# The last head's steps of a two-layer hybrid backbone, placed ahead of the products that fill TensorE's time

## The chip, the cores and the metric

One Trainium2 chip, one core of it. The metric is the device time of one execution in microseconds (us), as the median of some runs. The profile is of one execution.

## What is computed

Two layers over 256 context tokens and 512 latent tokens of 1024 channels. Layer 0 is a gated linear recurrence with 16 heads in both directions (HGRN2), layer 1 a scanned recurrence with a short convolution (RG-LRU). Each layer normalises, applies a modulation, widens, mixes, gates with SiLU and adds a gated projection back to the stream. Cut to layer 0:

```
h  = rms(x, norm_g) * (1 + scale) + shift            # 768 x 1024, context and latent
q, v, zf, zb, g = split(h @ w_in, 5)                 # 16 heads of 128 each
f  = lb + (1 - lb) * sigmoid(z);  k = 1 - f          # per direction
S  = diag(prod f) S + (k * decay)^T v                # chunk by chunk, carried state
o  = scores(q, k, decay) v + (q * decay) S           # forward plus backward
r  = rms(o, norm_g_head) * silu(g)                   # per head
x  = x + gate * (concat_heads(r) @ w_out)            # context and latent
```

Layer 1 starts from the mean square of every channel of the new x, so all 16 heads' projections must be in x before it begins.

## The kernel before, in words

The stream x stays in SBUF as `x1`, channels on the partitions: 8 blocks of 128 channels by 768 tokens. Products that need full precision are done as three fp32r products, high by high, high by low and low by high; `mm3` (L307) issues them, and `Weights.split` (L118) makes the high part of each weight tile on ScalarE (L129) and the low part on VectorE (L130), from pools of three buffers each.

**One head of layer 0** is a generator, `hgrn(h, side)` (L429). `prep` (L418) has made `kd`, `QQ` and the first `kt` from the head's projections. Then come:

- `dg`, the diagonal products (L442), and seven levels. At each, VectorE multiplies `KK` in place by decay products (L502), forms the next decays `T` (L507) and multiplies `QQ` in place (L509); ScalarE gathers the next `kt` from `KK` and, at odd levels, `qt` from `QQ` (L416, L490, L491); TensorE makes the score products `lv` (L460) of 32 or 64 columns; VectorE puts the low levels' scores into `D` under a mask (L468).
- Transposes of `KK` (L519), state products `U` (L533), the state chain `S` on VectorE (L541), the outputs `o` (L565).
- The norm of the head and the gate. Heads 0 to 14 take the mean by a product with ones (L580) and a reciprocal on VectorE (L588 to L590). Head 15 goes through `rstd_of` (L255): `msv` (L262), `rv` (L265, L266), `rbv` (L272), with L593 and L595 on VectorE.
- The result, split into `rhi` and `rlo` (L598 to L604; named `r` for head 14, which uses another pool).

`rhi` and `rlo` stand in a pool with one buffer for each parity of the head: head 15's `rhi` takes the buffer of head 13's.

**The fill.** While one head's chain runs, TensorE is kept busy with other products: the projections of the next head (`in_item`, L358) and output products of earlier heads (`out_item`, L391). `interleave` (L156) takes one step of the chain, adds its weight, and emits fill until the fill's share of its total has caught up. For head 15 the fill is `in_item(15, 3)`, the gate projection of head 15 itself (two halves, evacuated by a sigmoid at L337 and a multiply at L341), and `out_item((12, 13, 14))`: 16 items, each of nine products of 384 columns in one PSUM bank: three for head 12, three for 13, three for 14. An add on VectorE (L405, `x <- o`) takes each into `x1` and frees the bank. All fill takes its PSUM from `dps`, four banks; the chain takes its from `aps`, four others. The output products of head 15 alone follow behind the loop (`out_item((15,))`, L730), then the norm of layer 1 (`msh`, L262) and its first projections (`rc`, `rl`).

**What sets the order.** Nobody writes the engines' queues by hand. Every instruction has a number, its place in program order, and the planner fills each engine's queue in the order of its own timing model: at each moment the engine gets, of the instructions that the model has ready, the one with the lowest number. Buffers of a pool are given out in the order in which the program asked for them. `tc.high_priority(n)` takes n from the numbers of what is emitted inside and puts the counter back on leaving. The kernel before uses it for the weight splits (100, L128) and, in layer 1, for some evacuations. On the chip each engine then runs its queue in order, with semaphores between engines.

Of the kernel before, what the change touches and what calls it, by code (L numbers as in the profile page):

```python
# [20 lines left out]
NH = 16  # L21
# [129 lines left out]
def run_all(gen):  # L151
    for _ in gen or ():
        pass


def interleave(main, weight, filler, total):  # L156

    done, n = 0.0, 0.0
    for w in main:
        n += w  # L160
        while filler is not None and done < total * min(1.0, n / weight):
            try:
                done += next(filler)
            except StopIteration:
                filler = None
    run_all(filler)


def build(tc, ins, out, plan):
# [188 lines left out]
    def in_item(h, ty):  # L358
        w = wget("in", h, ty)
        in_tiles(h, ty)  # L360
        for half, c in enumerate(halves):
            ps = dtile(f"in{h}_{ty}_{half}")[:, :HN]
            mm3(ps, hpairs(w, c, range(4)), last=False)
            yield 1960.0
            mm3(ps, hpairs(w, c, range(4, 8)), first=False)
            in_evac(h, ty, half, ps)
            yield 1960.0

    def v_item(g):
        for u in range(2):  # L370
            st[2 * g + u]["V"] = vp.tile([P, NC, P], F32, name=f"V{2 * g + u}", tag="V")
        pss = [dtile(f"v{g}_{b}") for b in range(3)]
        for part in range(2):
            whi, wlo = (w.rearrange("p (k e) -> p k e", k=4) for w in wget("v", g, part))
            for c in range(NC):
                t = slice(P * c, P * c + P)
                ps = pss[c // 2][:, 256 * (c % 2):256 * (c % 2) + 256]
                for k in range(4):
                    kk = 4 * part + k
                    for i, (xh, w) in enumerate(((h_hi, whi), (h_hi, wlo), (h_lo, whi))):  # L380
                        PE.matmul(ps, lhsT=xh[:, kk, t], rhs=w[:, k],  # L381
                                  start=part == 0 and k == 0 and i == 0 and c % 2 == 0,
                                  stop=part == 1 and k == 3 and i == 2 and c % 2 == 1, skip_group_check=True)
                if part == 1 and c % 2 == 1:
                    b = c // 2
                    src = pss[b].rearrange("p (c e) -> p c e", c=2)
                    for u in range(2):
                        A.activation(st[2 * g + u]["V"][:, 2 * b:2 * b + 2], src[:, :, P * u:P * u + P], AF.Copy)
                yield 1300.0

    def out_item(heads, accs=None, done=None):  # L391
        ws = [wget("out", h) for h in heads]
        gate = ada[0][:, 2]
        parts = segs if accs else halves
        order = [(d, i) for d in range(DK) for i in range(2)]
        for d, i in sorted(order, key=lambda x: x[1]) if accs else order:
            e = slice(P * d, P * d + P)
            c = parts[i]
            ps = dtile(f"o{heads[0]}_{d}_{i}")[:, :c.stop - c.start]
            mm3(ps, [(w[0][:, e], w[1][:, e], st[h]["r"][0][:, c], st[h]["r"][1][:, c]) for h, w in zip(heads, ws)])  # L400
            for j, g in enumerate(segs):
                a, b = max(c.start, g.start), min(c.stop, g.stop)
                if a < b:
                    xs = x1[:, d, a:b]
                    V.scalar_tensor_tensor(xs, ps[:, a - c.start:b - c.start], gate[:, d, 1 - j:2 - j], xs,  # L405
                                           ALU.mult, ALU.add)
            if accs:
                sumsq(accs, THREE, lambda n: ktp.tile([P, NT], F32, name=n, tag="kt"), d, c)
                if d == DK - 1:
                    done(i)  # L410
            yield 490.0 * len(heads)
# [6 lines left out]
    def prep(h):  # L418

        s = st[h]  # L420
        QQ = s["QQ"] = qqp.tile([P, 2, NT], F32, name=f"QQ{h}", tag="QQ")
        kd = s["kd"] = kdp.tile([P, NT], F32, name=f"kd{h}", tag="kd")
        kt = s["kt"] = ktp.tile([P, NT], F32, name=f"kt{h}_0", tag="kt")
        V.tensor_tensor(kd, s["KK"][:, 0], s["KK"][:, 1], ALU.add)
        gather(s["KK"], kt, 1)
        V.tensor_tensor(QQ[:, 0], s["q"], s["T0"][:, 1], ALU.mult)
        V.tensor_tensor(QQ[:, 1], s["q"], s["T0"][:, 0], ALU.mult)
# [179 lines left out]
    HW = 1.5 + 28.0 - 6.3 + 1.5 + 3.0 + 3.6 + 0.5 + 7.0  # L607
# [83 lines left out]
    def chain_(gens):  # L691
        for g in gens:
            yield from g

    def head_in(h):
        outs = out_item((h - 3, h - 2)) if h % 2 and h >= 3 else None
        yield from in_item(h, 0)
        yield from in_item(h, 1)
        yield from in_item(h, 2)
        prep(h)  # L700
        if h % 2 == 0:
            yield from v_item(h // 2)
        if h < NH - 1:
            yield from outs or ()
            yield from in_item(h, 3)

    def extra(h):
        if h in (1, 2):
            return [ada_block(0, 3 + h)]
        return [ada_block(1, h - 10)] if h >= 10 else []  # L710

    for h in range(NH):
        if h == 0:
            fill, total = [v_item(0), in_item(0, 3), head_in(1)], 54700.0
        elif h < NH - 1:
            fill, total = [head_in(h + 1)], 45300.0 if h < NH - 2 else 23500.0
        else:
            fill, total = [in_item(h, 3), out_item((h - 3, h - 2, h - 1))], 31400.0
        side = chain_(extra(h + 1) if h < NH - 1 else [])
        interleave(hgrn(h, side), HW, chain_(fill), total)  # L720
        run_all(side)
    accs1 = [pl.tile([P, n], F32, name=f"acc1_{i}", tag=t)[:, :NT]
             for i, (pl, t, n) in enumerate(((kdp, "kd", NT), (qp, "q", NT), (sp, "S", 2 * (NC - 1) * P)))]
# [306 lines left out]
```

## Time and profile before

| what | value |
|---|---|
| median of 3 runs | 1586.57 us (1585.46 to 1586.60) |
| the profiled execution, own time | 1585.53 us |
| its span in the profile | 1583.7 us |
| TensorE busy | 1530.8 us, 97% |
| VectorE busy | 1208.6 us, 76% |
| ScalarE busy | 903.9 us, 57% |
| granted TensorE clock, mean | 0.986 |
| share of TensorE in the chain that ended last | 87% |

The profile times start at the first instruction. A line of the timeline gives the start, the duration, the engine, the line of the kernel, the output and inputs by tile name, the number of merged instructions and, in brackets, the idle time of the engine just before and what ended it. On TensorE each 384-column product is shown with its full length of 0.34 us, but such products start some 0.17 us apart. Four-byte products of the chain are shown as two instructions each. The granted clock (PEclk) is 1.00 at 2.4 GHz and 0.50 at 1.2 GHz.

### The profile page before, as it was taken

To read this page: it belongs to the slowest core of one execution; us is meant where nothing else is said; L and a number is where in the kernel's file an instruction comes from. 1 tells how busy PE (TensorE), PEld (TensorE's weight loads), DVE (VectorE), ACT (ScalarE), POOL (GpSimd) and SP (SyncE) were. 2 spreads that over 40 slices of the span, in tenths; PEclk is the share of its full clock that TensorE was granted. 3 is DMA by queue.
4 is the path that set the end of the run, shared out by engine and by line. 5 is a ranking of instruction groups with operands and counts; after the bars stand their busy time and mean duration, and the time that the engine had idled before them with its cause. 6 is when DMAs were issued, how large, how long until landed. Compare 5 with 4: busy or idle time off the path is not lost.

```text
span 1583.7 us, 34061 instructions
## 1 busy us (share of the span) xinstructions
PE 1530.8 (97%) x14740; PEld 1429.7 (90%) x14740; DVE 1208.6 (76%) x1867; ACT 903.9 (57%) x1423; POOL 11.8 (1%) x16
## 2 busy tenths in 40 slices
PE   5999999999999999999999999998999999999995
PEld 3899999999999999999999999987888888888884
DVE  4767678768867878767866876787668797797898
ACT  4554554555544554554445555654578577667874
POOL 0000000000000000000000000001000000000001
PEclk9999999999999999999999999998999999999997
DMA  8231211111211211223222131201222212221211
GB/s 317 91 121 54 95 55 41 55 54 30 80 41 42 68 45 51 81 69 103 70 92 73 54 120 56 94 15 54 66 68 67 89 59 67 94 78 59 76 54 53
DMA packets 33861, 116.80 MB, mean 74 GB/s; under 512 B 3632, under 2 KB 6064, under 8 KB 33712
## 3 DMA queue, kind: packets, MB, share of 16 engines
q1 hardware_dynamic: 32192, 113.26, 22.5%
q8 instruction: 116, 1.90, 0.5%
q10 hardware_dynamic: 1520, 1.37, 0.3%
q14 instruction: 33, 0.27, 0.1%
HBM read 112.52 MB, written 2.10 MB: 72 GB/s over the span
## 4 chain that ended last, share of the span: by engine, by line
PE 87%; DVE 8%; ACT 2%; issue 1%; POOL 0%; DMA 0%; POOLq 0%; DVEq 0%; ACTq 0%
PE in L311 12%; PE in L312 11%; PE in L313 11%; PE v L381 9%; PE lv L460 4%; PE o L565 4%; PE r L313 3%; PE r L311 3%; PE r L312 3%; PE o L311 3%; PE o L312 3%; PE o L313 3%; PE U L533 2%; PE gt L311 2%; PE gt L312 2%; PE gt L313 2%
## 5 line engine op out<-in xcount | busy, mean ns | idle before, releaser
L311 PE MATMUL in<-h_hi,hi 128*128 128x384 f32 x1024 | 350.4, 343 | 3.4 <-ACT h_hi L304 2.8
L312 PE MATMUL in<-h_lo,hi 128*128 128x384 f32 x1024 | 345.8, 338 | 0.3 <-DVE h_lo L305 0.3
L313 PE MATMUL in<-h_hi,lo 128*128 128x384 f32 x1024 | 344.6, 337 | 0.0
L130 DVE TENSOR_TENSOR lo<-raw,hi 128x1024 fp32r<-128x1024 f32 x160 | 195.8, 1225 | 85.9 <-ACT hi L129 85.6
L129 ACT ACTIVATE hi<-raw 128x1024 fp32r<-128x1024 f32 x160 | 168.1, 1057 | 110.5 <-PE in L312 49.3
L311 PEld LDWEIGHTS in<-h_hi,hi 128*128 128x128 f32 x1024 | 192.9, 189 | 16.8 <-issue 9.9
L312 PEld LDWEIGHTS in<-h_lo,hi 128*128 128x128 f32 x1024 | 193.1, 189 | 2.8 <-issue 1.6
L313 PEld LDWEIGHTS in<-h_hi,lo 128*128 128x128 f32 x1024 | 192.6, 188 | 0.8 <-issue 0.4
L509 DVE TENSOR_TENSOR QQ<-QQ,T 128x768 f32<-128x768 f32 x112 | 117.7, 1051 | 20.7 <-ACT qt L491 20.5
L313 PE MATMUL r<-h_hi,lo 128*128 128x512 f32 (+1 forms) x344 | 123.8, 360 | 3.8 <-DVE lo L130 3.8
L416 ACT ACTIVATE kt<-KK 128x768 f32<-128x768 f32 x112 | 102.5, 915 | 40.8 <-DVE KK L502 33.1
L502 DVE TENSOR_TENSOR KK<-KK,T 128x768 f32<-128x768 f32 x112 | 117.3, 1047 | 9.7 <-ACT kt L416 8.2
L312 PE MATMUL r<-h_lo,hi 128*128 128x512 f32 (+1 forms) x344 | 123.1, 358 | 0.0
L311 PE MATMUL r<-h_hi,hi 128*128 128x512 f32 (+1 forms) x344 | 123.0, 358 | 0.0
L337 ACT ACTIVATE sg<-in 128x384 f32<-128x384 f32 x128 | 61.5, 482 | 100.7 <-PE in L313 100.5
L381 PE MATMUL v<-hi,h_hi 128*128 128x256 f32 x384 | 111.3, 290 | 0.0
L381 PE MATMUL v<-hi,h_lo 128*128 128x256 f32 x384 | 107.4, 280 | 0.0
L381 PE MATMUL v<-lo,h_hi 128*128 128x256 f32 x384 | 107.3, 279 | 0.0
L588 DVE RECIPROCAL sq<-sq 128x384 f32<-128x384 f32 x30 | 76.3, 2546 | 21.1 <-ACT sq L582 20.9
L405 DVE SCALAR_TENSOR_TENSOR x<-o,ada,x 128x256 f32<-128x256 f32 (+1 forms) x184 | 82.1, 486 | 11.3 <-PE o L313 10.8
L311 PE MATMUL o<-rhi,hi 128*128 128x384 f32 (+2 forms) x240 | 85.3, 357 | 1.8 <-DVE lo L130 1.2
L311 PE MATMUL gt<-xh,hi 128*128 128x384 f32 x256 | 85.6, 337 | 0.8 <-ACT xh L790 0.4
(207 smaller groups left out, 3280.1 us busy)
## 6 DMA issues: line engine op xcount, KB each, us to landing
raw<-in_hgw_dram SPq DMA_DIRECT2D x64, 512.0 KB, 3.6
raw<-in_ada_dram SPq DMA_DIRECT2D x48, 512.0 KB, 3.8
raw<-in_rgi_dram SPq DMA_DIRECT2D x32, 512.0 KB, 3.9
raw<-in_hgv_dram SPq DMA_DIRECT2D x16, 512.0 KB, 3.5
raw<-in_hgo_dram SPq DMA_DIRECT2D x16, 512.0 KB, 3.6
raw<-in_rgg_dram SPq DMA_DIRECT2D x16, 512.0 KB, 3.6
raw<-in_rgo_dram SPq DMA_DIRECT2D x16, 512.0 KB, 3.9
x<-in_x_dram SPq DMA_DIRECT2D x8, 384.0 KB, 5.9
```

Source lines behind the costliest of these rows:

```text
L129: self.nc.scalar.activation(hi, r, AF.Copy)
L130: self.nc.vector.tensor_tensor(lo, r, hi.bitcast(F32), ALU.subtract)
L311: PE.matmul(ps, lhsT=wh, rhs=xh, start=first and i == 0, stop=False, skip_group_check=skip)
L312: PE.matmul(ps, lhsT=wh, rhs=xl, start=False, stop=False, skip_group_check=skip)
L313: PE.matmul(ps, lhsT=wl, rhs=xh, start=False, stop=last and i == n - 1, skip_group_check=skip)
L381: PE.matmul(ps, lhsT=xh[:, kk, t], rhs=w[:, k], start=part == 0 and k == 0 and i == 0 and c % 2 == 0, stop=part == 1 and k == 3 and i == 2 ...
L405: V.scalar_tensor_tensor(xs, ps[:, a - c.start:b - c.start], gate[:, d, 1 - j:2 - j], xs, ALU.mult, ALU.add)
L416: A.activation(view(kt, 0, [[2 * B, n], [B, 2], [1, B]]), view(KK, 0, [[2 * B, n], [NT + B, 2], [1, B]]), AF.Copy)
L460: PE.matmul(ps[w * g:w * g + w, w * c:w * c + w], lhsT=kt[:, o:o + w], rhs=rhs, start=c == 0, stop=c == NC - 1, skip_group_check=True, til ...
L502: V.tensor_tensor(kv, kv, view(T, 1, [[2, n], [m - 1, 2], [0, B]]), ALU.mult)
L509: V.tensor_tensor(qv, qv, view(T, m + 1, [[2, n], [-m - 1, 2], [0, B]]), ALU.mult)
L588: V.reciprocal(rs, rs)
```

## The change

A new generator wraps the head's generator and takes each of its steps inside `tc.high_priority(2000)`. It is used for head 15 alone. The fill of head 15, everything of head 14, the projections and `prep` of head 15 and the weight splits keep their numbers. No instruction is added, removed or resized.

```diff
+    def ahead_of_fill(gen):
+
+        while True:
+            with tc.high_priority(2000):
+                w = next(gen, None)
+            if w is None:
+                return
+            yield w
+
@@
         side = chain_(extra(h + 1) if h < NH - 1 else [])
-        interleave(hgrn(h, side), HW, chain_(fill), total)
+        interleave(hgrn(h, side) if h < NH - 1 else ahead_of_fill(hgrn(h, side)), HW, chain_(fill), total)
         run_all(side)
```

## Rows read from the trace of the kernel before

**Rows 1.** The page: TensorE and VectorE; busy us, share, instructions.
```profile
PE 1530.8 (97%) x14740; PEld 1429.7 (90%) x14740; DVE 1208.6 (76%) x1867; ACT 903.9 (57%) x1423; POOL 11.8 (1%) x16
```

**Rows 2.** Stretches: length; PE, PEld, DVE, ACT, POOL busy (instructions); PEclk; DMA share, GB/s.
```profile
1030.30:1035.00 4.70, 4.47 (x114) 3.76 (x113) 4.66 (x6) 4.47 (x6) 0.00 (x0) 1.00 0.01 3
1035.00:1040.00 5.00, 3.06 (x69) 2.49 (x71) 5.00 (x8) 2.43 (x4) 0.00 (x0) 1.00 0.34 97
1040.00:1045.00 5.00, 4.08 (x112) 3.68 (x113) 5.00 (x12) 1.73 (x3) 0.00 (x0) 1.00 0.03 11
1045.00:1056.00 11.00, 11.00 (x170) 9.77 (x169) 10.89 (x24) 7.15 (x15) 0.00 (x0) 1.00 0.01 1
1060.00:1075.57 15.57, 15.57 (x109) 15.15 (x107) 6.88 (x19) 3.98 (x7) 0.00 (x0) 1.00 0.01 2
1075.57:1080.00 4.43, 1.73 (x10) 1.32 (x10) 4.43 (x6) 3.06 (x4) 0.00 (x0) 0.99 0.53 143
1080.00:1084.00 4.00, 3.98 (x17) 3.47 (x17) 4.00 (x9) 2.62 (x7) 2.67 (x3) 0.59 0.47 156
1091.00:1104.00 13.00, 10.29 (x49) 9.76 (x48) 9.88 (x18) 5.90 (x11) 2.28 (x2) 0.61 0.11 40
```

**Rows 3.** VectorE by line, 1029.4 to 1056 us; busy us, mean ns, idle.
```profile
L509 DVE TENSOR_TENSOR QQ<-QQ,T 128x768 f32<-128x768 f32 x7 | 7.3, 1049 | 0.1
L502 DVE TENSOR_TENSOR KK<-KK,T 128x768 f32<-128x768 f32 x7 | 7.3, 1045 | 0.0
L405 DVE SCALAR_TENSOR_TENSOR x<-o,ada,x 128x256 f32<-128x256 f32 (+2 forms) x14 | 6.0, 470 | 0.0
L507 DVE TENSOR_TENSOR T<-T 128x768 f32<-128x768 f32 (+6 forms) x7 | 2.6, 379 | 0.0
L468 DVE COPY_PREDICATED D<-masks,lv 128x192 f32<-128x192 uint8 x5 | 1.8, 365 | 0.0
L341 DVE SCALAR_TENSOR_TENSOR gs<-in,prm,sg 128x384 f32<-128x384 f32 x2 | 1.2, 603 | 0.0
L130 DVE TENSOR_TENSOR lo<-raw,hi 128x1024 fp32r<-128x1024 f32 x1 | 1.2, 1202 | 0.0
L604 DVE TENSOR_TENSOR r<-sq,r 128x384 fp32r<-128x384 f32 x1 | 0.9, 909 | 0.0
```

**Rows 4.** VectorE's timeline: start us, us, line, op, out<-in.
```profile
1029.44 0.94 DVE L424 TENSOR_TENSOR kd<-KK 128x768 f32<-128x768 f32 x1
1030.77 1.63 DVE L502 TENSOR_TENSOR KK<-KK,T 128x768 f32<-128x768 f32 x1
...
1035.87 1.20 DVE L130 TENSOR_TENSOR lo<-raw,hi 128x1024 fp32r<-128x1024 f32 x1
...
1055.06 1.26 DVE L405 SCALAR_TENSOR_TENSOR x<-o,ada,x 128x384 f32<-128x384 f32 x3
...
1073.34 0.69 DVE L595 TENSOR_TENSOR gs<-gs,rbv 128x512 f32<-128x512 f32 x1 [1.41 <-PE rbv L272]
```

**Rows 5.** TensorE's timeline, 1036 to 1079 us.
```profile
1036.84 0.63 PE L460 MATMUL lv<-qt,kt 128*32 128x32 f32 x48 [1.59 <-ACT qt L416]
1037.39 0.61 PE L313 MATMUL o<-r,lo 128*128 128x384 f32 x2
...
1075.06 0.34 PE L312 MATMUL o<-r,hi 128*128 128x384 f32 x1
1075.23 0.34 PE L313 MATMUL o<-r,lo 128*128 128x384 f32 x1
...
1078.23 0.38 PE L312 MATMUL o<-rlo,hi 128*128 128x256 f32 x1 [0.86 <-DVE rlo L599]
```

**Rows 6.** ScalarE's timeline.
```profile
1041.26 0.85 ACT L416 ACTIVATE kt<-KK 128x768 f32<-128x768 f32 x1 [1.92 <-DVE KK L502]
...
1074.39 2.00 ACT L129 ACTIVATE hi<-raw 128x1024 fp32r<-128x1024 f32 x2 [2.67 <-PE o L312]
1076.30 0.40 ACT L598 ACTIVATE rhi<-gs 128x256 fp32r<-128x256 f32 x1
```

## The prediction, made before the change was run

> **What bounds the kernel now.** I read the engines' shares first: TensorE is busy 97% of the span, VectorE 76% [rows 1]. So an edit pays only where TensorE stands idle, and the place to look is the stretch of head 15. The view of busy time by stretch [rows 2] shows three parts. From 1030.3 to 1045 TensorE is idle 0.23 + 1.94 + 0.92 = 3.1 us, while VectorE is full. From 1045 to 1056 and from 1060 to 1075.57 TensorE is full. From 1075.57 to 1080 it works 1.73 of 4.43 us.
>
> Next, what ends the first part. VectorE by line [rows 3] has two kinds of work in it. The chain of head 15: 7.3 + 7.3 + 2.6 + 1.8 = 19.0 us. The rest are things that the fill needs: the last steps of head 14's result (L590, L604), the low part of head 14's output weights (L130), the gate multiply that empties the two banks of head 15's gate projection (L341), and the adds that empty the output banks (L405). All eleven lines of that view (L424, L589 and L590, 1.9 us together, are not shown) make 30.2 us in 26.6 us of time, because neighbours overlap; so a listed microsecond costs 0.88.
>
> Last, what ends the stretch. The last fill product starts at 1075.23 and ends at 1075.57 [rows 5], and head 15's last multiply is over at 1073.34 + 0.69 = 1074.03 [rows 4], before it. Two things of the tail wait for the fill, not for the chain. Head 15's `rhi` takes head 13's buffer, which the fill reads to its last item, and it runs at 1076.30 [rows 6]. And the split of head 15's output weights takes head 12's buffer; it starts at 1074.39 after a wait for an output product [rows 6]. **So a chain that is done earlier lets nothing start earlier.** The stretch ends when TensorE has done its fill, and its end moves by what TensorE's idle time before that does.
>
> **What the change moves.** No work is added. The four windows from 1030.3 to 1056 and the one from 1060 hold 574 TensorE and 69 VectorE instructions [rows 2]; 2000 is more than twice that, so head 15's steps go ahead not of the fill alone but of everything that is left of head 14 and of the weight splits, on TensorE, VectorE and ScalarE alike, wherever they are ready. On POOL and in the DMA queue the chain has nothing; no weight load moves by itself, but each one waits for the split that frees its buffer, and those go back with the rest.
>
> *VectorE.* The chain's first multiply needs `kd` (L424), which is not raised: it ends about 1030.3 [rows 4]. From there the chain's 19.0 us take 19.0 x 0.88 = 16.7 us if nothing comes between: the levels end near 1047.0, against the 1055.06 at which the adds behind the last level start now [rows 4]. Does anything come between? A gather is 0.85 us [rows 6] and stands between two multiplies of `KK`, which with the 0.95 of the multiply and some 0.1 us for each hand-over makes 2.0 us a level; VectorE's own work is 16.7 / 7 = 2.4 us a level on average, somewhat less at the last levels, where `T` is small. So VectorE has hardly a gap before the last levels, and L590, L604, L130 and most of L341 wait till then. This is the step on which the forecast rests.
>
> *TensorE.* Of an output item the first six products need heads 12 and 13 only; the third three need head 14's result, and its low product also the weights' low part: today two such products stand behind L130 until 1037.39 [rows 4, 5]. Of the four banks two are held by the gate projection until L341 has run for each half. So with VectorE withheld, the fill has 2 banks x 6 products, 0.17 us apart [rows 5], that is 2.1 us. The chain's own products are eight bundles, 0.63 us each [rows 5], 5.0 us in all. From 1031.3 to 1047 that is 7.1 us of work in 15.7 us: idle 8.6. Bounds: the 3.1 us of today if VectorE finds room for the fill's helpers after all (0 more; less than that is rival A), and 8.6 us (5.5 more). I take 8.0, since some helpers slip in at the last levels: 8.0 - 3.1 = **+4.9 us**. Behind the levels the transposes, states and outputs of head 15 cover the (0.9 + 1.2 + 1.2) x 0.88 = 2.9 us that VectorE then needs for L604, L130 and L341 [rows 3]; if that cover fails, it is up to 2.9 us more.
>
> *The waits that go.* The 1.59 us in front of the score product [rows 5] is a wait for the chain; it is inside the 3.1 us subtracted above.
>
> *The clock.* Behind the stretch with 1.73 us of work in 4.43, the granted clock is 0.59 over 4 us [rows 2], that is 0.41 / 0.5 x 4 = 3.3 us at the lower of the two levels, 1.2 GHz. From 1091 it is 0.61 over 13 us, 10.1 us at the lower level [rows 2]. From 1035 to 1040, with 3.06 of 5 us busy, it stayed at 2.4 GHz. While TensorE starves, the lower level costs little; behind that, where its queue is full again, it costs half of the time that it lasts: bounds 0 and 10.1 / 2 = 5 us. The row of 1080 is the nearest, as it too follows a few microseconds of broken work, and I take half of its 3.3 us: **+1.7 us**. The Trainium skill ("TensorE: Matmul & The Clock Gate", Part 1, What's actually happening) says that the throttled state is the default and that activity releases it; by that the loss is certain and the time 1592.7, by the row of 1035 there is none and the time 1591.0. The rows of 1080 and 1091 are with the page.
>
> *The tail.* ScalarE runs two splits (2.00 us) and then `rhi` [rows 6]; with the change `rhi` passes the second, 1.0 us sooner behind the end of the fill, and the 0.86 us wait for `rlo` [rows 5] shrinks. But the second split's VectorE half then stands in front of the adds that empty the banks. Bounds -1.0 and 0; I take **-0.5 us**.
>
> Sum: 4.9 + 1.7 - 0.5 = +6.1 us on the profiled execution's 1585.53 us: 1591.6. The median of the runs shown is 1.04 us above that execution; against it the forecast is **1592.7 us**, 0.4% slower. The times below are against the median too.
>
> **The rivals.** A: *the chain's lead counts*, faster. If head 14's result, the low part of its weights and the emptied gate banks stand in VectorE's queue before head 15's first multiply, the fill is fed throughout; the 3.1 us of idle time, which end mostly with chain steps, go, and the tail gives 1.0: -4.1, 1582.5 us. The point that decides is whether L604 and L130 come before L502's first. For it: the largest of today's gaps, 1.59 us, ends with a gather of the chain [rows 5], which then comes sooner. Against it: L130 is at 1035.87 now, behind that multiply at 1030.77 [rows 4], and the change only pushes it back. The Trainium skill ("Perfetto Trace Analysis", Optimization Strategy) says to find the gaps on the engine one optimizes for and to make what ends them start sooner or finish faster; this rival is that rule at work, and it leaves out what the raised steps push back. Chance 0.10.
>
> B: *nothing that can be measured*, because VectorE has gaps enough (the gather paces the levels, 2.0 us against 2.4 is not far), or because the order is fixed by readiness and 2000 changes little: idle 3.1 us as now, tail -0.5 to 0: 1586.1 to 1586.6 us. Chance 0.16.
>
> C: *the clock stays low* through the transposes, states, outputs and much of the fill: with twice the 10.1 us of 1091 to 1104 at the lower level it costs +10.1 instead of +1.7, 1601.1 us. The row of 1091 is for it, the 3.3 us at 1080 against it [rows 2]. Chance 0.08.
>
> **How the numbers follow.** The forecast has 0.66, and reaches from the least that counts as slower to 5.5 + 5 + 0 us, 1597.1. A measurement of this kernel can tell about 0.2%, 3.2 us, from no change. Slower than that: the forecast and C, 0.74. Within: B, 0.16. Faster: A, 0.10. The range reaches from 1586.0, B's time, to 1600.0, just short of C.
>
> **What would show it.** In the changed kernel's trace: L502 seven times by about 1047 with hardly an L405 between; L604 of `r` and L130 of head 14's weights behind 1040; TensorE some 40 to 60% busy between 1032 and 1046 with score products alone; a granted clock below 1 somewhere from 1035 to 1060; the last fill product near 1081; head 15's last multiply near 1060, 20 us before `rhi`. It is wrong if L604 stays near 1032, or if TensorE is as full as now in 1030 to 1045.

## The result, and the profile after

| | before | after |
|---|---|---|
| median of 6 runs each | 1585.51 us (1583.69 to 1586.60) | 1597.06 us (1595.32 to 1598.21) |
| ratio, 95% interval | | 1.007 [1.006, 1.008] |
| the profiled execution, own time | 1585.53 us | 1598.0 us |
| its span | 1583.7 us | 1596.2 us |
| TensorE busy | 1530.8 us | 1537.6 us |
| granted clock, mean | 0.986 | 0.981 |
| last fill product starts | 1075.23 | 1086.34 |
| first `rc` product of layer 1 starts | 1096.04 | 1108.96 |

The change made the kernel 11.5 us slower; 6.1 had been forecast. Of the 12.9 us by which the profiled execution is late at layer 1, 11.1 are there when the fill ends.

The page's first part of the changed kernel, where [rows 1] has 1530.8 and 1208.6: TensorE is busy 6.8 us longer with as many instructions, so not all of the loss is idle time.

```profile
PE 1537.6 (96%) x14740; PEld 1434.6 (90%) x14740; DVE 1210.0 (76%) x1867; ACT 903.4 (57%) x1423; POOL 11.8 (1%) x16
```

Stretches of the changed kernel, the columns as in [rows 2]: length, then TensorE, its weight loads, VectorE, ScalarE and POOL busy, granted clock, DMA share, GB/s.

```profile
1030.30:1035.00 4.70, 2.65 (x59) 2.04 (x58) 4.63 (x7) 3.44 (x5) 0.00 (x0) 0.96 0.28 94
1035.00:1040.00 5.00, 4.73 (x105) 4.19 (x105) 5.00 (x8) 4.07 (x6) 0.00 (x0) 0.50 0.06 20
1040.00:1045.00 5.00, 2.19 (x160) 1.87 (x148) 4.79 (x9) 2.51 (x4) 0.00 (x0) 0.84 0.01 3
1045.00:1050.00 5.00, 2.87 (x67) 2.18 (x58) 4.65 (x7) 4.35 (x11) 0.00 (x0) 0.50 0.02 3
1050.00:1055.00 5.00, 5.00 (x24) 3.96 (x23) 0.69 (x2) 1.93 (x6) 0.00 (x0) 0.50 0.00 0
```

Three things are to be seen. TensorE is idle 2.05 + 0.27 + 2.81 + 2.13 = 7.3 us from 1030.3 to 1050, where it was 3.1 [rows 2]. The clock is at its lower level, 1.2 GHz, in most of 1035 to 1055, where it was at 2.4 GHz throughout. And from 1050 to 1055 TensorE is full with 24 instructions, while VectorE does 0.69 us of work: something else than VectorE makes it slow there.

VectorE's timeline of the changed kernel (start, duration, engine, line, operation, out<-in, count, idle time before), where [rows 4] has the first `L502` at 1030.77:

```profile
1031.06 1.23 DVE L130 TENSOR_TENSOR lo<-raw,hi 128x1024 fp32r<-128x1024 f32 x1
1032.21 1.59 DVE L502 TENSOR_TENSOR KK<-KK,T 128x768 f32<-128x768 f32 x1
1033.65 0.53 DVE L590 TENSOR_TENSOR sq<-sq,gs 128x384 f32<-128x384 f32 x1
1034.11 0.93 DVE L426 TENSOR_TENSOR QQ<-q,T 128x768 f32<-128x768 f32 x1
...
1046.53 0.95 DVE L502 TENSOR_TENSOR KK<-KK,T 128x768 f32<-128x768 f32 x1
1047.40 0.95 DVE L509 TENSOR_TENSOR QQ<-QQ,T 128x768 f32<-128x768 f32 x1
1048.27 0.86 DVE L604 TENSOR_TENSOR r<-sq,r 128x384 fp32r<-128x384 f32 x1
1049.03 0.62 DVE L341 SCALAR_TENSOR_TENSOR gs<-in,prm,sg 128x384 f32<-128x384 f32 x1
...
1060.21 1.26 DVE L405 SCALAR_TENSOR_TENSOR x<-o,ada,x 128x256 f32<-128x256 f32 x3
```

The seven `L502` stand between 1032.21 and 1046.53 with no add (`L405`) between them. Head 14's last `L604` goes from 1032.44 to 1048.27, the first add from 1042.48 to 1060.21.

TensorE's timeline of the changed kernel. The first two lines are waits for the chain; the next four are score products of the last level and state products, taking turns; the last two are the end of the fill and head 15's first product with `rlo`, which [rows 5] has at 1075.23 and 1078.23:

```profile
1043.27 0.63 PE L460 MATMUL lv<-qt,kt 128*32 128x32 f32 x48 [2.21 <-ACT qt L416]
...
1046.95 1.28 PE L460 MATMUL lv<-qt,kt 128*32 128x32 f32 x48 [1.77 <-ACT qt L490]
...
1055.21 0.33 PE L460 MATMUL lv<-QQ,kt 128*64 128x64 f32 x2
1055.47 0.49 PE L533 MATMUL U<-V,KK 128*128 128x128 f32 x2
1055.89 0.33 PE L460 MATMUL lv<-QQ,kt 128*64 128x64 f32 x2
1056.15 0.49 PE L533 MATMUL U<-V,KK 128*128 128x128 f32 x2
...
1086.34 0.34 PE L313 MATMUL o<-r,lo 128*128 128x384 f32 x1
...
1088.20 0.38 PE L312 MATMUL o<-rlo,hi 128*128 128x256 f32 x1 [0.67 <-DVE rlo L599]
```

And ScalarE's at the end of the fill: the split of head 15's weights has waited 17.32 us for the fill's products, and `rhi` runs behind it, 16 us after the chain's last multiply (1070.39).

```profile
1085.49 1.06 ACT L129 ACTIVATE hi<-raw 128x1024 fp32r<-128x1024 f32 x1 [17.32 <-PE o L312]
1086.46 0.40 ACT L598 ACTIVATE rhi<-gs 128x256 fp32r<-128x256 f32 x1
```

### The profile page after: what moved, and what is told of

The parts are those of the page before. It is cut to its first block, busy times and chain, and to the rows that moved or that the text cites. A ratio compares the mean times of both kernels' runs of the same rounds, so it can differ in the third digit from the quotient of the medians.

```text
span 1596.2 us, 34068 instructions
## 1 busy us (share of the span) xinstructions
PE 1537.6 (96%) x14740; PEld 1434.6 (90%) x14740; DVE 1210.0 (76%) x1867; ACT 903.4 (57%) x1423; POOL 11.8 (1%) x16
## 4 chain that ended last, share of the span: by engine, by line
PE 87%; DVE 8%; ACT 3%; issue 1%; DMA 1%; POOL 0%; POOLq 0%; DVEq 0%; ACTq 0%
PE in L311 12%; PE in L312 11%; PE in L313 11%; PE v L381 9%; PE lv L460 4%; PE o L565 4%; PE r L313 3%; PE r L311 3%; PE r L312 3%; PE o L311 3%; PE o L312 3%; PE o L313 3%; PE U L533 2%; PE gt L311 2%; PE gt L312 2%; PE gt L313 2%
## 5 line engine op out<-in xcount | busy, mean ns | idle before, releaser
L130 DVE TENSOR_TENSOR lo<-raw,hi 128x1024 fp32r<-128x1024 f32 x160 | 196.0, 1226 | 85.8 <-ACT hi L129 85.5
L509 DVE TENSOR_TENSOR QQ<-QQ,T 128x768 f32<-128x768 f32 x112 | 117.9, 1053 | 20.7 <-ACT qt L491 20.5
L502 DVE TENSOR_TENSOR KK<-KK,T 128x768 f32<-128x768 f32 x112 | 117.8, 1051 | 9.7 <-ACT kt L416 8.2
L405 DVE SCALAR_TENSOR_TENSOR x<-o,ada,x 128x256 f32<-128x256 f32 (+1 forms) x184 | 82.4, 488 | 19.0 <-PE o L313 18.6
```

What stands on the lines that cost most here:

```text
L130: self.nc.vector.tensor_tensor(lo, r, hi.bitcast(F32), ALU.subtract)
L502: V.tensor_tensor(kv, kv, view(T, 1, [[2, n], [m - 1, 2], [0, B]]), ALU.mult)
L509: V.tensor_tensor(qv, qv, view(T, m + 1, [[2, n], [-m - 1, 2], [0, B]]), ALU.mult)
```

## The experiments

The theory behind the prediction: the raised levels take VectorE from what the fill needs, TensorE starves, and the lower clock adds to it. The rivals: the loss comes from the raised steps behind the levels; it comes from one overtaken piece only; or the clock costs nothing. All runs stand in one table. The comparisons ran on different chips, so "above before" and the ratio are each against the kernel before in the same comparison, and runs of different comparisons are compared by these. The fill's end is the start of its last product in the profiled execution, the idle time is the sum of the windows from 1030.3 to 1050.

| run | us | above before | ratio, 95% interval | fill's end | TensorE idle |
|---|---|---|---|---|---|
| before | 1585.5 | | | 1075.23 | 3.1 |
| the change | 1597.06 | 11.6 | 1.007 [1.006, 1.008] | 1086.34 | 7.3 |
| e1, levels | 1593.72 | 8.9 | 1.0051 [1.0037, 1.0065] | 1081.39 | 8.6 |
| e2, behind the levels | 1598.12 | 13.3 | 1.0077 [1.0063, 1.0091] | 1087.71 | 1.5 |
| e4, levels written first | 1592.07 | 7.2 | 1.0039 [1.0025, 1.0053] | 1080.76 | 7.9 |
| e3, ten products more | 1598.12 | 13.3 | 1.0076 [1.0062, 1.0091] | 1086.07 | 2.2 |
| e7, numbers in a row | 1595.03 | 10.2 | 1.0065 [1.0053, 1.0078] | 1084.37 | 9.5 |
| e10, e7 and four products | 1594.74 | 9.9 | 1.0064 [1.0051, 1.0076] | 1083.12 | 5.9 |
| e8, behind the levels, in a row | 1586.59 | 1.8 | 1.0005 [0.9996, 1.0014] | 1075.07 | 3.1 |
| e11, e7 and helpers raised | 1591.45 | 6.6 | 1.0047 [1.0035, 1.0060] | 1081.50 | 5.9 |
| e14, e11 and adds raised | 1586.81 | 1.5 | 1.0011 [1.0002, 1.0020] | 1074.40 | 1.2 |
| e5, before, free buffers | 1587.27 | 2.0 | 1.0011 [1.0002, 1.0020] | 1075.39 | 3.1 |
| e16, e8, free buffers | 1585.11 | -0.2 | 1.0000 [0.9991, 1.0009] | 1075.98 | 3.1 |
| e15, e14, free buffers | 1586.85 | 1.5 | 1.0009 [1.0000, 1.0017] | 1074.61 | 1.2 |

### Two halves, and a price that nobody had looked for

e1 raises the first seven steps, e2 those behind them; e2's line has `7 <= i < 99`.

```diff
-        while True:
-            with tc.high_priority(2000):
+        for i in range(99):
+            with tc.high_priority(2000 if 0 <= i < 7 else 0):
                 w = next(gen, None)
```

> Only the seven levels of head 15 are raised by 2000; its transposes, states, outputs and result keep their own priority. Theory 1 (the levels starve the fill, and the clock falls behind that): nearly the whole loss stays, 9 to 12 us above the kernel before, TensorE idle some 7 us from 1030 to 1050 and the last fill product 9 to 11 us late. Rival (the loss is made by the raised steps behind the levels, which mix with the last level's score products and stand ahead of the adds): 0 to 3 us above the kernel before.

> Only the steps behind the seven levels are raised by 2000. Theory 1: the fill is fed as before, the last fill product stays within 1 us of 1075.2, the time within 1.5 us of the kernel before, and a lead of the chain's last multiply (1074.0 before) of a few us brings nothing. Rival (the raised steps behind the levels make the loss): 6 to 12 us above the kernel before.

e1 kept most of the loss, 8.9 us, just under the 9 to 12 of theory 1; its fill ended 6.2 us late, where 9 to 11 had been expected. e2 lost 13.3 us, though its TensorE was idle only 1.5 us and its clock was at 2.4 GHz from 1030 to 1090. The edit had done something that was not meant. `tc.high_priority` puts the counter back on leaving, with an argument of 0 too; so each step left as it was and the fill behind it got the same numbers, and the planner queued them in turns. A stretch and three lines of e2's TensorE:

```profile
1055.00:1060.00 5.00, 5.00 (x35) 2.93 (x35) 1.61 (x3) 0.84 (x1) 0.00 (x0) 1.00 0.01 3
```

```profile
1055.11 0.45 PE L311 MATMUL o<-rhi,hi 128*128 128x384 f32 x1
1055.48 0.25 PE L460 MATMUL lv<-QQ,kt 128*32 128x32 f32 x2
1055.66 0.45 PE L312 MATMUL o<-rlo,hi 128*128 128x384 f32 x1
```

One fill product and one score product (two instructions) take 1055.66 - 1055.11 = 0.55 us. In a row a fill product takes 0.17 us, and a bundle of 24 score products 0.56 (1043.44 to 1044.00 in this run), 0.02 each: the turn costs 0.36 us. e2 has 39 such turns in three levels, 14.0 us; 1.6 us of idle time go, and the fill ended 12.5 us late. That sum closes, so here the turns alone made the loss. The busy share hides them: TensorE is shown full. The weight loads show them, 2.93 us of 5. The Trainium skill ("Perfetto Trace Analysis", Identifying the Most-Contended Engine) says that TensorE's busy share is no measure of how near it is to its limit and sends the reader to the rate of floating-point work and the share of weight loads. This row agrees: 5.00 of 5 us busy, 2.93 of weight loads.

So neither e1 nor e2 is a clean half of the change: e1's steps behind the levels take turns with the fill too. But they showed where to look. In the change the raised steps share numbers with one another: each starts near the number at which the one before began, and the last level's score products were queued between transposes and state products.

### Numbers in a row

```diff
             ...
+                off = 2000
+                if plan is not None and at is not None:
+                    off = tc.cur_priority - at
+                with tc.high_priority(off):
+                    w = next(gen, None)
+                    at = tc.cur_priority
```

> The changed kernel, but the raised steps get numbers one behind the other; in the changed kernel each step begins again near the number of the one before it, so that the last level's score products were queued one by one between the transposes and state products (1048.5 to 1058.5). Theory 1 (of the 11 us at the end of the fill, about 5 are starvation, 3.3 the lower clock from 1048.5 to 1055 and 2.6 this alternation): 2 to 3 us below the changed kernel, 1594 to 1595.5. Rival (TensorE waits for the chain there anyway): 1597 as the changed kernel.

> Only the steps behind the seven levels are raised, with numbers one behind the other, and the levels keep their own numbers, which are no longer shared with the fill. Theory 1: the fill is fed as before, last fill product within 1 us of 1075.2, time within 1.5 us of the kernel before although the chain's last multiply ends some us earlier. Rival (raising what stands behind the levels costs as well): 3 us or more above the kernel before.

e7 is the change with this alone, e8 uses it for the steps behind the levels and leaves the levels outside any such block. e7's bundles are whole again:

```profile
1051.66 1.55 PE L460 MATMUL lv<-QQ,kt 128*64 128x64 f32 x24
...
1055.34 2.40 PE L533 MATMUL U<-V,KK 128*128 128x128 f32 x20
```

Its fill ends 2.0 us sooner than the change's. The medians are of two comparisons: 10.2 us above the kernel before against 11.6, which is 1.3 us and less than the 2 to 3 expected, and the two ratio intervals overlap; so the rows carry this step, not the medians. In the changed kernel one score product of 64 columns and one state product took 1055.89 - 1055.21 = 0.68 us. In the kernel before they stood in bundles, and these lines, which follow one another there in time, give 0.85 / 12 = 0.07 and 1.34 / 6 = 0.22 us:

```profile
1053.21 0.92 PE L460 MATMUL lv<-QQ,kt 128*64 128x64 f32 x24
1054.06 0.44 PE L311 MATMUL o<-r,hi 128*128 128x384 f32 x1
...
1056.65 1.58 PE L533 MATMUL U<-V,KK 128*128 128x128 f32 x12
1057.99 0.42 PE L313 MATMUL o<-rhi,lo 128*128 128x384 f32 x1
```

e8, the clean second half, is the kernel before within its interval: the chain's last multiply came at 1067.81 instead of 1074.03, and nothing followed from it. So the loss comes with the raised levels.

### What the levels overtake

e4 raises nothing; it writes the levels out ahead of the fill, so that they pass the fill's helpers but not head 14.

```diff
+    def levels_first(gen):
+        yield sum(next(gen) for _ in range(NLEV))
+        yield from gen
...
+        interleave(main if h < NH - 1 else levels_first(main), HW, chain_(fill), total)
```

> No priority is raised; the seven levels of head 15 are written out ahead of the first fill item, so they go ahead of the fill and of its helpers (the gate multiply, the adds, the weight splits), but not of head 14's last steps, of head 15's own preparation or of splits asked for earlier. Theory 1a (it is the overtaken rest of head 14, above all the last part of its result, that starves the fill): L604 of r stays near 1032 to 1034, the time is within 2 us of the kernel before. Theory 1b (it is the overtaken gate multiply and adds, that is the output banks): 6 to 11 us above the kernel before.

The last part of `r` was made at 1031.82, and the loss was still 7.2 us by the medians: theory 1a falls. VectorE's lines of e4 show what came late: the gate multiply, the first adds, and also the low part of head 14's weights. So e4 does not part the output banks from these weights; e11 and e14 do.

```profile
1031.82 0.93 DVE L604 TENSOR_TENSOR r<-sq,r 128x384 fp32r<-128x384 f32 x1
...
1046.25 1.22 DVE L130 TENSOR_TENSOR lo<-raw,hi 128x1024 fp32r<-128x1024 f32 x1
...
1049.20 1.13 DVE L341 SCALAR_TENSOR_TENSOR gs<-in,prm,sg 128x384 f32<-128x384 f32 x2
1050.25 1.25 DVE L405 SCALAR_TENSOR_TENSOR x<-o,ada,x 128x256 f32<-128x256 f32 x3
```

e11 and e14 go the other way: the whole chain stays raised, with its numbers in a row, and the helpers are raised above it. e11:

```diff
+            with tc.high_priority(2300) if (h, ty) == (NH - 1, 3) else nullcontext():
+                in_evac(h, ty, half, ps)
...
+            if h == NH - 2:
+                up.enter_context(tc.high_priority(2300))
             g = s["gs"][:, c]
...
+        with tc.high_priority(2300) if h == NH - 1 else nullcontext():
+            prep(h)
```

and the splits of heads 13 and 14 in the same way. e14 adds:

```diff
+                    with tc.high_priority(2300) if len(heads) == 3 else nullcontext():
+                        V.scalar_tensor_tensor(xs, ps[:, a - c.start:b - c.start], gate[:, d, 1 - j:2 - j], xs,
+                                               ALU.mult, ALU.add)
```

> The kernel with numbers one behind the other, and with what the fill waits for raised above the chain: head 14's last steps (to L604 of its r), head 15's preparation, the gate multiply of head 15's gate projection (L341 before) and the splits of the weights of heads 13 and 14. The adds behind the output products are not raised. Theory 1 (the chain starves the fill by overtaking these): r is ready by 1034, TensorE's idle time from 1030 to 1050 falls to about that of the kernel before (3 to 4 us), the clock stays up, and the time is within 3 us of the kernel before. Rival (it is the adds, that is the output banks, or VectorE's time as such): 5 us or more above the kernel before.

> As the run with the raised helpers (1591.5), and the adds that empty the output banks of the fill raised above the chain too. Theory 1 (what is left there of the loss are the banks that wait for their adds behind the chain): TensorE idles 3 to 4 us from 1030 to 1050, the last fill product is back near 1076 to 1078, and the time within 2 us of the kernel before. Rival (VectorE lost time in the order as such, with the chain's own products of T far ahead of kd): still 4 us or more above the kernel before.

e11 had the low part of head 14's weights at 1032.07 and the last part of `r` at 1033.22, won 3.6 us against e7 and was still 6.6 us above the kernel before: its rival, not theory 1. Some of TensorE's waits in e11 point at what was left; its file is some lines longer, and `L410` and `L345` there are `L405` and `L341` before:

```profile
1038.24 0.41 PE L315 MATMUL o<-rhi,hi 128*128 128x384 f32 x1 [1.39 <-DVE x L410]
...
1040.43 0.44 PE L315 MATMUL o<-rhi,hi 128*128 128x384 f32 x1 [0.37 <-DVE gs L345]
...
1050.49 0.44 PE L315 MATMUL o<-rhi,hi 128*128 128x384 f32 x1 [0.86 <-DVE x L410]
```

The adds. These waits are a part only, since the longest one in this stretch, 1.85 us at 1049.38, ends with a gather of the chain; e14 is what settles it. With the adds raised too, e14 has TensorE idle 1.2 us, less than before the change, and the fill ends 0.8 us sooner than before the change:

```profile
1035.00:1040.00 5.00, 4.78 (x121) 4.14 (x113) 5.00 (x8) 4.27 (x6) 0.00 (x0) 1.00 0.06 20
1040.00:1045.00 5.00, 4.89 (x116) 4.52 (x117) 5.00 (x10) 1.27 (x2) 0.00 (x0) 1.00 0.02 3
```

So the starvation is shown: 1.5 us of the loss (0.1%) are left when what the fill waits for is raised above the chain. By the medians above the kernel before, and in this order of adding, the adds were worth 5.1 us (e11 to e14), the helpers 3.6 (e7 to e11) and the turns 1.3 (the change to e7); the adds were not raised alone.

It does not follow that a raised chain is free. The last `L502` of the kernel before and of e14 (`L508` there):

```profile
1053.04 0.96 DVE L502 TENSOR_TENSOR KK<-KK,T 128x768 f32<-128x768 f32 x1
...
1056.62 0.96 DVE L508 TENSOR_TENSOR KK<-KK,T 128x768 f32<-128x768 f32 x1 [0.41 <-ACT kt L422]
```

The levels of e14 are 3.6 us later than before the change: the adds and helpers took back on VectorE what the change had given to the levels. Only behind the levels does the chain lead, by 2.0 us at its last multiply (1071.99).

### The clock

e3 adds ten unread products to the change, two ahead of each score bundle of levels 1 to 5; e10 adds four to e7, ahead of levels 3 and 5. They do work that no result needs. The lines are e10's.

```diff
+        def busy(ps, src):
+            for i in range(2):
+                PE.matmul(ps[:, 192:512], lhsT=src[:, :P], rhs=src[:, 256 * i:256 * i + 320], start=True, stop=True,
+                          skip_group_check=True)
...
+                if h == NH - 1 and l > 1:
+                    ps_ = atile(f"lv{h}_{l}")
+                    busy(ps_, kt)
```

> The changed kernel with ten products added that nobody reads, 128x320 in 32-bit floats, two ahead of each score bundle of levels 1 to 5 in columns of its bank that are not used, some 0.5 us each. They keep TensorE busy where it waited for the chain and change nothing else. Theory 1 (of the 11.5 us some 4 are idle time and some 7 the lower clock): the granted clock stays at 1.00 or near it from 1035 to 1055, and the time falls by 4 to 7 us against the changed kernel, to 1590 to 1593. Rival (the fill is late because its helpers on VectorE are late; the clock only fell where nothing was to be done): the time stays at 1597 or grows by up to 3 us, even if the clock stays up.

> The kernel with numbers one behind the other, and four products that nobody reads, 128x320, two in front of the score products of level 3 and two of level 5, some 0.6 us each at the higher clock, where TensorE stood idle for 2.2 and 1.8 us. Theory 1 (the lower clock behind 1045 is worth 3.3 us): granted clock near 1.00 from 1045 to 1055 and 2.5 to 3.5 us less than the run without these products. Rival (the clock falls all the same, or what it slows has slack): within 1 us of the run without them, or slower by their 2.4 us.

e3 gained nothing, which is its rival's time, but tells little of the reason: at the lower level its first products took 1.44 us a piece, they stood among the score products, and the last `L502` moved from 1046.53 to 1052.91. What it may have won by the clock it lost by a later chain, and the two can't be parted. e10 left the chain alone (last `L502` 1046.59, e7 1046.90). Its stretches, where e7 has 0.98, 0.50 and 0.50:

```profile
1040.00:1045.00 5.00, 3.06 (x158) 2.21 (x148) 5.00 (x9) 2.88 (x4) 0.00 (x0) 1.00 0.01 3
1045.00:1050.00 5.00, 3.34 (x72) 2.18 (x62) 4.92 (x8) 3.48 (x8) 0.00 (x0) 0.92 0.00 0
1050.00:1055.00 5.00, 5.00 (x46) 4.09 (x46) 2.85 (x6) 3.43 (x11) 0.00 (x0) 0.74 0.01 3
```

The fill ended 1.25 us sooner than e7's. That is what the rows give: where TensorE's queue was full, from 1050.4 to 1055, e7 was at the lower level for all 4.6 us and e10 for some 2.2, and half of the difference is 1.2. But these are one execution each, and they differ ahead of the first added product too: from 1035 to 1040 the granted clock is 0.66 in e10 and 1.00 in e7. The median fell by 0.3 us only, which these intervals can't tell from nothing: behind the fill e10 stood longer at the lower level than e7. So the rows agree with a loss of half the time at the lower level, up to the fill's end; that the whole kernel gets it back is not shown.

### Would the lead count, if what follows were free?

In e5, e15 and e16 head 15's result goes into two free buffers of `V`, its weights into those of `T0` and `QQ`, so neither waits for the fill.

```diff
+        elif h == NH - 1:
+            rhi, rlo = [vp.tile([P, NT], F32R, name=f"r{n}{h}", tag="V") for n in ("hi", "lo")]
...
+    W.slots["out", NH - 1] = ((tp, "T0", 2 * NT), (qqp, "QQ", 2 * NT))
```

> The kernel before, no priority raised, but head 15's result goes into two buffers of V that are free and the two halves of its output weights into those of T0 and QQ, so that neither waits for the fill any more. Theory 1 (behind the fill two buffers are waited for, not the chain): rhi runs at about 1074, straight behind the last multiply (1074.0), its weights are split by 1070, the first product with rlo comes at about 1076 instead of 1078.2: 1.5 to 3 us faster, 1581.5 to 1583.5. Rival (the adds or the norm behind hold the end): within 0.5 us of the kernel before.

> The same free buffers, and the steps behind the seven levels raised with numbers one behind the other (alone this moved the last multiply from 1074.0 to 1067.8 and the time not at all). Theory 1 (a lead of the chain counts only where what follows has its buffers): rhi and rlo are done before the fill ends, no gap behind the fill, 1 to 2 us faster than the free buffers alone. Rival (the lead is hidden all the same): within 0.5 us of them.

> The whole chain raised, with what the fill needs raised above it, and with the free buffers for head 15's result and weights. Theory 1: the fill is fed and the chain's lead counts: 2 to 5 us faster than the same without the free buffers, at or below the kernel before. Rival: the lead is hidden, within 1 us of the same without the free buffers.

None beat the kernel before. The wait for the buffers did go: e5's first product with `rlo` is at 1075.68, 2.5 us sooner than before, behind the fill without a gap. Then TensorE waited for other things:

```profile
1078.47 0.39 PE L311 MATMUL o<-rhi,hi 128*128 128x256 f32 x1 [1.68 <-DVE x L405]
...
1081.17 0.39 PE L311 MATMUL o<-rhi,hi 128*128 128x256 f32 x1 [0.91 <-DVE x L405]
...
1083.83 0.87 PE L262 MATMUL msh<-cst,acc 128*128 128x1 f32 x4 [2.04 <-POOL acc L289]
```

The adds wait on VectorE behind three weight splits (`L130` at 1075.64, 1079.50 and 1081.03), and the mean square of layer 1 waits for POOL's sums. The last product of head 15 ended at 1093.0 in e5 and at 1091.6 before. The same two kinds of wait stand in e15 and e16, the one for POOL's sums with 2.03 us in both. So the prediction's sentence "the stretch ends when TensorE has done its fill" holds only up to 1075; behind it the adds and POOL's sums come last, with a lead of the chain or without. Which of the two would have to go for a gain was not tried.

The lead itself is not worth nothing everywhere. e16 is 2.2 us below e5 by the medians, about what its theory 1 had said (1 to 2), and the means of their eleven runs differ by 2.0 us (95%: 0.8 to 3.1). But e5 is as much above the kernel before, so the lead won back what the free buffers had cost, and no more; where, the traces can't tell, since e5's is of its fastest run and e16's of its slowest. e15 won nothing against e14.

## Why the prediction was right, and which terms were off

**Direction and place: right.** Slower, by VectorE's order in 1030 to 1050, with the chain's lead useless behind it. e14 shows the first, e8 the second.

**VectorE's order: right in kind, with two pieces misplaced.** Seven `L502` by 1047 without an add between them, and `L604` behind them, came as forecast. But the low weights (`L130`) came ahead of the first `L502`, at 1031.06, not behind 1040; and `L426` of head 15's own preparation, not raised, was pushed to 1034.11 and held the first score products. The rival's point of decision, "whether L604 and L130 come before L502's first", was the wrong one: in e11 both came before it, and the kernel still lost 6.6 us. What was left there were the adds that empty the output banks. The prediction had the banks in its sum (two banks of six products) but not in its test. It also read two products at 1037.39 as held by `L130`; they stand right behind a score bundle that itself had waited 1.59 us for `qt` [rows 5], so that `L130` held them is not shown.

**The +4.9 us of idle time: right in size.** 7.3 - 3.1 = 4.2 in the changed kernel, 4.8 in e4, 6.4 in e7. In the changed kernel nine fill products within the starved stretch ran at the lower level, 1036.14 to 1039.31, 3.2 us for what takes 1.6; by this reckoning the other 1.6 would have been idle time. Together 5.8 us, a little over the upper bound of 5.5. Between 1032 and 1046 TensorE was busy 8.05 of 14 us, within the forecast 40 to 60%, but with twelve fill products in it and not score products alone; twelve are what the prediction's two banks of six give.

**The clock, +1.7 us: too small by half.** From 1048.50 to 1055 TensorE had a full queue at the lower level, 6.5 / 2 = 3.25 us. The prediction took the row of 1080 as its nearest; the change made two stretches of broken work and not one, and the clock fell within a wait of 2.24 us (at 1034.7) and again at 1044.9, behind one of 2.21. The bounds (0 to 5) held. The Trainium skill ("TensorE: Matmul & The Clock Gate", Part 1, What's actually happening), by which the loss was certain, agrees with these rows, and with e4, whose clock fell behind a stretch with 1.25 of 5 us busy. Why the kernel before kept 2.4 GHz from 1035 to 1040 [rows 2] they do not tell.

**The term that was missing: the turns.** From 1048.50 to 1058.54 the changed kernel does the last scores, transposes and state products in 10.0 us. At 2.4 GHz and in bundles they take 0.85 + 1.09 + 2.23 = 4.2 us by the rows of the kernel before. The lower clock is 3.25 of the difference, the turns the other 2.6, and in e7 the fill ended 2.0 sooner. The rule was in the document before the prediction: the counter is put back on leaving. That steps raised one after the other then share their numbers was not drawn from it.

The sum at the end of the fill is 5.8 + 3.25 + 2.6 = 11.6 us, and 11.1 were measured: the last fill product at 1086.3, not near 1081. The forecast time was 1592.7 us; 1597.06 is the very end of what its own terms reach to (1597.1). That it stayed within the range is in part luck: the room up there was meant for the clock, and the turns, which no term had, and a tail of the other sign took it up.

**The tail, -0.5 us: right in its order, wrong in what it brings.** The product with `rlo` comes 1.9 us behind the last fill product instead of 3.0, as forecast, and the adds wait behind the second split, as forecast: 1.83 us in front of TensorE instead of 0.66. From the fill's last product to the first `rc` it was 20.81 us before and 22.62 after, outside the bounds. But of the runs with the same steps there e7 and e11 have 20.77 and 20.80, e8 and e10 have 22.94. What goes with it is how long the clock stays down from the wait for the adds on: some 3.4 us in e7, 10.2 in e10. Two stretches of e8, whose fill ended when that of the kernel before did:

```profile
1080.00:1085.00 5.00, 5.00 (x21) 4.26 (x20) 4.43 (x10) 3.15 (x8) 2.99 (x3) 0.50 0.70 211
1085.00:1090.00 5.00, 5.00 (x19) 4.08 (x18) 2.59 (x4) 0.63 (x1) 0.00 (x0) 0.61 0.00 1
```

and the second of them in the kernel before:

```profile
1085.00:1090.00 5.00, 5.00 (x27) 4.24 (x28) 3.62 (x7) 2.15 (x5) 0.65 (x1) 1.00 0.01 3
```

So the 1.1 us that the order won there were spent on the clock in that execution; over eleven runs of e8 there is nothing to be told from the kernel before.

**The last multiply near 1060: wrong by 10 us**, 1070.39. The turns held the state products, and the last `L509` came at 1059.09; but in e7, where the bundles are whole, the last multiply is at 1066.86, so the turns are some 3.5 of the 10 us and the rest is open. It cost nothing, as `rhi` waited until 1086.46.

**The rivals.** A (the lead counts) had the wrong condition. The rule named with it, of the Trainium skill ("Perfetto Trace Analysis", Optimization Strategy), to make what ends a gap start sooner, is what e14 did for the right pieces: it closed the gaps (1.2 us idle), and still did not pay: its fill ended 0.8 us sooner and its first `rc` came 1.2 us later than before (1097.26), with the waits for adds and POOL's sums in between. B fell with the result. C's low clock came, 17 us of it, but some 10 of them in the stretch where TensorE starved.

## What to carry to other kernels

Before raising a chain, list on every engine what it passes, and ask of each passed piece who waits for it: here it was above all the adds that empty the other work's PSUM banks, and raising these and the other helpers took all but 0.1% of the loss away, and the levels' lead with it. After moving priorities, look at the queue itself for two kinds of products taking turns; the busy share does not show it, the count of instructions and the weight loads in a stretch do. And a chain that ends 6 us earlier, as in e8, gains nothing as long as something else is late next; here that was a buffer, then adds behind weight splits, then POOL.

## What the runs showed of the hardware

Products of different shape that take turns on TensorE are dear: 0.36 us for each turn between a product of 384 columns and a score product of 32 columns (128*32 in the trace), 0.39 us between a score product of 64 columns and a state product of 128 (0.68 against 0.07 + 0.22), all at 2.4 GHz. Turns between products that are both 128*128 in the trace are cheap: in e1 a transpose and a fill product took 0.29 us together, where 0.11 and 0.17 are their prices in a row. That score products are two instructions each does not explain the price: so are state products, and in e1 a state product and a fill product that take turns need 1063.16 - 1062.76 = 0.40 us, where 0.22 and 0.17 are their prices.

```profile
1059.27 0.27 PE L519 MATMUL kT<-cst,KK 128*128 128x128 f32 x1
1059.30 0.42 PE L312 MATMUL o<-rlo,hi 128*128 128x384 f32 x1
1059.56 0.27 PE L519 MATMUL kT<-cst,KK 128*128 128x128 f32 x1
```

The granted clock behind the same wait for the adds came back sooner in some profiled executions than in others, 2.2 us apart at layer 1, with the same products in the same order on TensorE (e7 and e10). What decides it stays open.
